# Head norms with tokens on the partitions, a new order of steps, and a regrouped recurrent mixer, in a two-layer streaming encoder trunk

## The chip, the cores and the metric

One core of a Trainium2 chip runs the whole program in one launch. The metric is the device time in microseconds (us) from start to end of one execution. Engines: TensorE (PE; its weight loads are shown as PEld), VectorE (DVE), ScalarE (ACT), GpSimd (POOL) and SyncE (SP), whose queue issues nearly all transfers.

## The reference, cut to what matters

Input is x of 512 tokens by 1024 channels. Two layers follow; each is half a SwiGLU feed-forward block (width 2816), a mixer, and another half block, all behind an RMS norm. The first layer's mixer ("even") runs eight attention heads of 64 beside eight RWKV-7 heads of 64; the second's ("odd") is a Griffin recurrent block of width 1280.

```python
for l in range(DEPTH):                       # DEPTH = 2
    x = x + 0.5 * swiglu(rmsnorm(x, ...), ...)
    h = rmsnorm(x, norm_mix[l])
    if l % 2 == 0:
        oa = chunk_attention(qa, ka, va, att_rel_bias[i])
        ob, v_b = rwkv7_group(pb, ...)
        x = x + jnp.concatenate([oa, ob], axis=-1) @ ab_w_out[i]
    else:
        x = x + rglru_block(h, ...)
    x = x + 0.5 * swiglu(rmsnorm(x, ...), ...)

# rwkv7_group, the two norms over the 64 channels of a head:
kk = _heads(k * k_k)
kk = kk * lax.rsqrt(jnp.maximum(jnp.sum(kk * kk, axis=-1, keepdims=True), 1e-24))
...
var = jnp.mean(jnp.square(o - mean), axis=-1, keepdims=True)
o = (o - mean) * lax.rsqrt(var + GN_EPS)
o = (o * ln_w + ln_b + jnp.sum(rh * kh * r_k, axis=-1, keepdims=True) * vh) * g

# rglru_block:
gate, xb = jnp.split(h @ w_in, 2, axis=-1)
gate = gelu(gate);  xc = conv4(xb) + conv_b
r = sigmoid(xc @ wa + ba);  ig = sigmoid(xc @ wx + bx)      # block-diagonal
a = exp(-8 * r * softplus(-lam));  mult = sqrt(1 - a * a)
hs = scan of  h_t = a_t * h_(t-1) + mult * ig * xc
return (hs * gate) @ w_out
```

## The kernel before, in words

**Layout.** Activations stand transposed: channels on the 128 partitions, the 512 tokens along the free axis, so a tile is 128x512. Every large product is made of three matmuls in a faster float format, on a high part and a remainder of each operand (`mm3`); the parts come from `split`: ScalarE copies the high part, VectorE subtracts it. Small products in the even mixer are plain float32 and appear as two matmul records each.

**Order of the program.** The phases are feed-forward 0, the even mixer (`ab`), feed-forward 1 and 2, the odd mixer (`rglru`), feed-forward 3. The compiler's planner orders each engine's instructions by program order and by when its model holds them ready. In the two mixers each TensorE instruction is pinned behind the one traced before it (`te.on`), so there TensorE's order is the written one, and the planner orders the other engines alone. Engines run their own queues in order. A tile's next use waits until the readers of the last one are done: PSUM has four banks under the name `mm` (projections, attention scores, transposes, outputs) and four under `aux` (small products).

**RMS norms.** `norm_square` squares each of the eight tiles of x and adds them up; `norm_end` sums over the partitions with a matmul of ones (`rms`), takes the root on ScalarE and the reciprocal on VectorE (`rsqrt`, lines 237 and 238). For the very first norm the squares are on GpSimd (line 222) and `norm_end` is called before the first feed-forward block; all other squares are on ScalarE (line 224).

**Even mixer.** Heads are worked in four pairs, numbers 0 to 3. Four strings give the written order: KEYS and VALUES (input projections, with the pairs' key preparation between), LEVELS (inverses of the triangular blocks) and ORDER (attention and the recurrence). A letter and a digit name a step and its pair; a number feeds so many units of a dense queue (in the first three the rest of the input projections, in ORDER the first half of the output projection), a unit being three 512-column matmuls; `k1:` feeds until that projection is done. The steps that matter here:

- `D` decay (line 532 on): LoRA products, sigmoids, a scan, exponentials; GpSimd forms `kah` from `a` (562), then VectorE turns `a` into (a-1)*k_a (563).
- `N` in KEYS (`pair_norm`, 573): one matmul of the squares with `blk`, a 128x128 matrix of two 64x64 blocks of ones, so that every partition of a head holds its sum (`kkn`); root, reciprocal of 128x512, then three VectorE products.
- `M` products of keys (`pair_lmat`), copied under a mask by VectorE (line 906); `T` token transposes of v; in ORDER `T`, `P`, `w`, `U`, `k`, `s`, `z`, `R`, `q`, `W` are the chunked recurrence of a pair.
- `N` in ORDER (`rwkv_norm`, 1070): matmul `gn_var` of the squares with `blk`, root (a table load and 512 columns on ScalarE), reciprocal, two VectorE products, GpSimd's product with the gate, and the split into `ob` (`mixed`).
- `A` and `B` (`att_probs`): scores of query blocks 0, 1 and 2, 3, each score tile in its own `mm` bank; reduction with the bias (line 711), exponential (717), reciprocal and scaling (720, 722). `B` ends with loading the next pair's query and key stacks. `C`, `E` (`att_turn`): transposes of the probabilities, copied back by ScalarE (735). `O`, `Y` (`att_out`): the products with v; `Y` ends with the split into `oa`.

**Odd mixer.** A loop of twenty projections (i = 0 to 19): ten give the branch that is convolved (`rg_conv`), ten the gate. Three projections later come that block's gates (`rg_gates`, sigmoids at line 1140). After the loop, for blocks 0 to 4 and then 5 to 9: tanh, exponential and square on ScalarE (1174 to 1177), two VectorE steps, then the root (1183), b = bx*m on GpSimd (1184), the scan on VectorE (1185), then GELU (1187), the product with the state (1188) and the split. The planner may start any of it earlier. The output projection (`cout`) follows, 240 matmuls.

Of the kernel before, what the change touches and what calls it, by code (L numbers as in the profile page):

```python
# [74 lines left out]
class Trunk:  # L75
# [3 lines left out]
    def __init__(self, ctx, tc, ins, out, first):  # L79
# [11 lines left out]
        self.n = 0  # L91
        self.jobs, self.parts_of, self.turn = [], {}, 0


# [157 lines left out]
    def ffn(self, li, next_gain):  # L252

        nc, tc = self.nc, self.tc
        wgu, wd = self.ins["gu"], self.ins["down"]
        xh, xl, rs = self.xh, self.xl, self.rs
        with tc.tile_pool(name=f"ffn{li}", bufs=1, reuse_waits="tile") as fp:
# [9 lines left out]
            for f in range(NF):  # L267
                pss = [self.mm_ps("gu") for _ in range(2)]
                both, at = [(0,), (1,)], None
                if self.early:  # L270


                    both, at = [(0, 1)], hbig.rearrange("p (a b) n -> p a (b n)", b=2)[:, 2:4]
                for ss in both:
                    parts = []
                    for s in ss:
                        place = at if s == 0 else None
                        parts.append(self.weights(wgu[li, f, s], D, at=None if place is None else (at[:, 0], at[:, 1])))
                    for k in range(KD):
                        c = slice(k * P, (k + 1) * P)  # L280
                        for s, (wh, wl) in zip(ss, parts):
                            self.mm3(
                                pss[s], wh[:, c], wl[:, c], xh[:, k], xl[:, k], k == 0, k == KD - 1
                            )
                g = fp.tile([P, NT], F32, tag="g", name=self.uid("g"), bufs=2)
# [40 lines left out]
    def ab(self, next_gain):  # L326
# [7 lines left out]
        with tc.tile_pool(name="ab", bufs=1, reuse_waits="tile") as rp:  # L334
# [3 lines left out]
            self.qkd = self.dp.tile([4, 2, 2, P, NT], F32, name="qkd")  # L338
            self.dec, self.kv, self.kk, self.vv, self.rr, self.pairs = ({} for _ in range(6))
            right = ExitStack()  # L340
            with tc.tile_pool(name="ab_in", bufs=1, reuse_waits="tile") as ep:
                self.later = None
                self.mtd = ep.tile([P, 32, 32], F32, tag="blocks", name="mtd")
                with tc.tile_pool(name="ab_keys", bufs=1, reuse_waits="tile") as kp:
# [15 lines left out]
                        "D": lambda p: self.rwkv_decay(p, rp, ep, kp),  # L360
                        "N": self.pair_norm,
                        "M": self.pair_lmat,
                        "T": lambda p: self.value_tokens(p, rp),
# [17 lines left out]
            with ExitStack() as st:  # L381
# [26 lines left out]
                    "W": lambda p: self.rwkv_out(p, sp),  # L408
                    "N": lambda p: self.rwkv_norm(p, rp),
                    "A": lambda p: self.att_probs(p, (0, 1), ap),  # L410
# [3 lines left out]
                    "O": lambda p: self.att_out(p, (0, 1)),  # L414
                    "Y": lambda p: self.att_out(p, (2, 3), rp),
                })
# [109 lines left out]
    def rwkv_decay(self, p, rp, ep, kp):  # L526
# [35 lines left out]
        nc.gpsimd.tensor_tensor(kah, a, kh, ALU.mult)  # L562
        nc.vector.tensor_scalar(a, a, -1.0, self.v("k_a", p), ALU.add, ALU.mult)
        self.dec[p] = kkt, rt, kh, kah, a
# [8 lines left out]
    def pair_norm(self, p):  # L573
        nc = self.nc
        kkt, rt, kh, kah, a = self.dec[p]
        k, kk, f = self.kv[p], *self.kk[p]
        ps = self.aux_ps("kkn")
        self.te.matmul(ps, self.blk, f, start=True, stop=True)
        self.rsqrt(f, ps, 1.0, 0.0)

        nc.vector.scalar_tensor_tensor(kk, f, 1e12, kk, ALU.min, ALU.mult)
        nc.vector.tensor_tensor(kkt, kk, kkt, ALU.mult)
        nc.vector.scalar_tensor_tensor(kah, kk, -1.0, kah, ALU.mult, ALU.mult)

    def pair_lmat(self, p):
# [5 lines left out]
        for q in range(4):  # L591
            q = slice(32 * q, 32 * q + 32)
            nc.scalar.activation(self.mtd[q, us], self.mt[q, us, q], AF.Copy)
        nc.vector.scalar_tensor_tensor(k2, k2, 1.0, self.kv[p], ALU.add, ALU.mult)
        nc.gpsimd.tensor_tensor(kh, k2, kh, ALU.mult)
# [92 lines left out]
    def att_probs(self, p, js, ap):  # L688
# [49 lines left out]

    def att_out(self, p, blocks, rp=None):

# [5 lines left out]
        for i in blocks:  # L746
            for h in range(2):
# [3 lines left out]
                )  # L751
        if rp:
            self.oa.append(self.mixed(rp, po, f"oa{p}"))

# [326 lines left out]

# [63 lines left out]
    def rglru(self, next_gain):  # L1145
        nc, tc = self.nc, self.tc
        self.te.on = True
        with tc.tile_pool(name="rg", bufs=1, reuse_waits="tile") as cp:
# [3 lines left out]
            rs_, bxs, ms, gs, yh, yl = [], [], [], [], [], []  # L1152
            convs = {}
            for i in range(2 * NR):
                n = i % NR
# [15 lines left out]
            for grp in (range(0, 5), range(5, 10)):  # L1171
                for n in grp:
                    m, a = slot("m", n), rs_[n]
                    nc.scalar.activation(m, a, AF.Tanh, scale=pos[:, n : n + 1])
                    nc.scalar.activation(a, a, AF.Exp, scale=neg[:, n : n + 1])
                    a2 = tmp("a2", 1)
                    nc.scalar.activation(a2, a, AF.Square)
                    nc.vector.tensor_scalar(a2, a2, 1.0, None, ALU.add)

                    nc.vector.scalar_tensor_tensor(m, m, 0.0, a2, ALU.max, ALU.mult)  # L1180
                    ms.append(m)
                for n in grp:
                    nc.scalar.activation(ms[n], ms[n], AF.Sqrt)
                    nc.gpsimd.tensor_tensor(bxs[n], bxs[n], ms[n], ALU.mult)
                    nc.vector.tensor_tensor_scan(bxs[n], rs_[n], bxs[n], 0.0, ALU.mult, ALU.add)  # L1185
                for n in grp:
                    nc.scalar.activation(gs[n], gs[n], AF.Gelu_apprx_tanh)
                    nc.vector.tensor_tensor(gs[n], gs[n], bxs[n], ALU.mult)
                    h, l = slot("r", n, F32R), slot("m", n, F32R)
                    self.split(h, l, gs[n])  # L1190
                    yh.append(h)
                    yl.append(l)
            self.norm_begin(next_gain)
# [85 lines left out]
def trunk_kernel(ctx: ExitStack, tc: tile.TileContext, ins: dict, out: bass.AP, phases="0A12C3"):  # L1279
# [97 lines left out]
```

## Time and profile before

| what | value |
|---|---|
| device time, median of 3 runs | 2000.65 us (1997.07 to 3977.45) |
| the profiled execution | 2000.92 us; its span 1999.2 us, 24418 instructions |
| TensorE busy | 1965.6 us (98%) |
| VectorE, ScalarE, GpSimd busy | 991.7, 770.3, 294.7 us (50, 39, 15%) |
| mean granted TensorE clock | 0.990 |
| HBM traffic | 258.30 MB read, 80.22 MB written |

The span is the time from the first to the last instruction. A busy TensorE is not TensorE at its peak: matmuls overlap, and a window's granted clock says which share of the full 2.4 GHz it had. "Idle before" is the time an engine did nothing before an instruction, and the name behind the arrow is the work whose end released it, as inferred from semaphores. Feed-forward 0 runs from 5 to 373 us, the even mixer to 720, feed-forward 1 and 2 to 1440, the odd mixer to 1626.

### The profile page before, as it was taken

Reading aid. Unit: us, or ns where it says so; the run is one execution under the profiler, and the core shown is the slowest. Engines: PE = TensorE matmul, PEld = TensorE weight load, DVE = VectorE, ACT = ScalarE, POOL = GpSimd, SP = SyncE. Lnnn points to the kernel's source line nnn. Section 1 sums busy time; section 2 is a strip of 40 time slices with the busy share of each in tenths; the row PEclk is TensorE's granted clock in tenths of the full one; section 3 lists DMA queues with packets and bytes.
Section 4 is the critical chain, followed back from the end, with each engine's and each line's share of the span. In section 5 each row is a group of like instructions: output and inputs, shape, how many; then the busy total and the mean of one; then the engine's idle time right before and its main releaser. Section 6 shows DMA issues by size and latency. Waiting matters only on the chain.

```text
span 1999.2 us, 24418 instructions
## 1 busy us (share of the span) xinstructions
PE 1965.6 (98%) x9642; PEld 1609.8 (81%) x9642; DVE 991.7 (50%) x1306; ACT 770.3 (39%) x1055; POOL 294.7 (15%) x216
## 2 busy tenths in 40 slices
PE   8999999999998999999999999999999999999998
PEld 6888888768776788888888888888888788888887
DVE  7655633378556465543335654433386544434332
ACT  5444422462245244422224442322279333222222
POOL 3111101112010021111000111101021211111100
PEclk9999999999998999999999999999999999999999
DMA  7999833534643469933335873233455442233332
GB/s 274 320 333 341 337 120 117 177 138 177 215 128 118 153 212 340 327 114 97 89 99 193 283 262 98 95 92 101 143 186 186 134 159 95 95 97 102 89 95 71
DMA packets 108930, 340.12 MB, mean 170 GB/s; under 512 B 12432, under 2 KB 15376, under 8 KB 108816
## 3 DMA queue, kind: packets, MB, share of 16 engines
q1 hardware_dynamic: 108672, 338.48, 50.2%
q8 instruction: 75, 1.23, 0.3%
q14 instruction: 39, 0.32, 0.1%
q10 hardware_dynamic: 144, 0.09, 0.0%
HBM read 258.30 MB, written 80.22 MB: 169 GB/s over the span
## 4 chain that ended last, share of the span: by engine, by line
PE 85%; DVE 7%; ACT 5%; issue 1%; DMA 1%; POOL 1%; SPq 0%; DVEq 0%; ACTq 0%; POOLq 0%
PE gu L69 47%; PE down L69 24%; PE proj L69 4%; PE cout L69 3%; PE outp L69 2%; DVE xc L1117 1%; PE prod L69 1%; DMA qkd<-qk 1%; DVE bx L1185 1%; DVE xblk L807 1%; DVE tblk L803 1%; PE wkv L69 1%; PE att_s L69 0%; ACT L1140 0%; PE w L69 0%
## 5 line engine op out<-in xcount | busy, mean ns | idle before, releaser
L141 ACT ACTIVATE whi<-raw 128x1024 fp32r<-128x1024 f32 (+2 forms) x269 | 277.6, 1032 | 787.9 <-PE gu L69 418.2
L69 PE MATMUL gu<-xh,wlo 128*128 128x512 f32 x1400 | 545.9, 390 | 1.0 <-DVE wlo L142 1.0
L69 PE MATMUL gu<-xl,whi 128*128 128x512 f32 x1400 | 545.5, 390 | 0.0
L69 PE MATMUL gu<-xh,whi 128*128 128x512 f32 x1400 | 545.5, 390 | 0.0
L142 DVE TENSOR_TENSOR wlo<-raw,whi 128x1024 fp32r<-128x1024 f32 (+2 forms) x269 | 322.8, 1200 | 243.5 <-ACT whi L141 240.2
L69 PEld LDWEIGHTS gu<-xh,wlo 128*128 128x128 f32 x1400 | 263.2, 188 | 56.6 <-DVE wlo L142 2.3
L69 PEld LDWEIGHTS gu<-xh,whi 128*128 128x128 f32 x1400 | 263.3, 188 | 54.8
L69 PEld LDWEIGHTS gu<-xl,whi 128*128 128x128 f32 x1400 | 263.2, 188 | 54.7
L289 POOL TENSOR_TENSOR s<-s,rs 128x512 f32<-128x512 f32 x88 | 153.9, 1749 | 801.7 <-ACT s L288 801.7
L69 PE MATMUL down<-hl,whi 128*128 128x512 f32 x558 | 217.2, 389 | 0.0
L69 PE MATMUL down<-hh,wlo 128*128 128x512 f32 x558 | 217.2, 389 | 0.0
L69 PE MATMUL down<-hh,whi 128*128 128x512 f32 x558 | 217.2, 389 | 0.0
L291 DVE TENSOR_TENSOR h<-gu,s 128x512 f32<-128x512 f32 x88 | 60.7, 690 | 207.8 <-PE gu L69 195.3
L286 DVE TENSOR_TENSOR g<-gu,rs 128x512 f32<-128x512 f32 x88 | 60.6, 690 | 164.1 <-PE gu L69 164.0
L227 POOL TENSOR_TENSOR ss<-ss,sq 128x512 f32<-128x512 f32 x36 | 53.7, 1492 | 486.7 <-ACT sq L224 486.7
L69 PEld LDWEIGHTS down<-hh,wlo 128*128 128x128 f32 x558 | 104.8, 188 | 21.7
L69 PEld LDWEIGHTS down<-hh,whi 128*128 128x128 f32 x558 | 104.8, 188 | 21.7
L69 PEld LDWEIGHTS down<-hl,whi 128*128 128x128 f32 x558 | 104.8, 188 | 21.6
L142 DVE TENSOR_TENSOR praw<-praw,phi 128x1024 f32<-128x1024 f32 (+2 forms) x75 | 87.2, 1164 | 58.7 <-ACT phi L141 58.0
L69 PE MATMUL proj<-xh,praw 128*128 128x512 f32 x336 | 114.0, 402 | 0.0
L141 ACT ACTIVATE phi<-praw 128x1024 fp32r<-128x1024 f32 (+2 forms) x75 | 72.1, 962 | 99.7 <-DMA praw<-in_cin_dram 39.8
L69 PE MATMUL down<-hbig,whi 128*128 128x512 f32 x248 | 76.9, 391 | 0.0
(439 smaller groups left out, 2329.0 us busy)
## 6 DMA issues: line engine op xcount, KB each, us to landing
raw<-in_gu_dram SPq DMA_DIRECT2D x174, 512.0 KB, 4.3
raw<-in_down_dram SPq DMA_DIRECT2D x64, 448.0 KB, 3.3
raw<-in_down_dram SPq DMA_DIRECT2D x32, 512.0 KB, 3.5
praw<-in_cin_dram SPq DMA_DIRECT2D x20, 512.0 KB, 5.4
parts_cin<-phi SPq DMA_DIRECT2D x20, 512.0 KB, 3.9
parts_cin<-praw SPq DMA_DIRECT2D x20, 512.0 KB, 5.1
praw<-parts_cin SPq DMA_DIRECT2D x20, 512.0 KB, 3.8
praw<-in_rw_dram SPq DMA_DIRECT2D x14, 512.0 KB, 6.1
```

What stands on the lines that cost most here:

```text
L69: return self.keep(self.tc.nc.tensor.matmul(*a, **k))
L141: nc.scalar.activation(hi, src, AF.Copy)
L142: (lo_eng or nc.vector).tensor_tensor(lo, src, hi.bitcast(F32), ALU.subtract)
L227: eng.tensor_tensor(self.ss, self.ss, sq, ALU.add)
L286: nc.vector.tensor_tensor(g, pss[0], rs, ALU.mult)
L289: nc.gpsimd.tensor_tensor(s, s, rs, ALU.mult)
L291: nc.vector.tensor_tensor(h, pss[1], s, ALU.mult)
L803: nc.vector.tensor_tensor(t, l[:, j + 1 :, j : j + 1].to_broadcast([P, n, c]), x[:, j : j + 1, 0:c].to_broadcast([P, n, c]), ALU.mult,)
L807: nc.vector.tensor_tensor(x[:, j + 1 :, 0:c], x[:, j + 1 :, 0:c], t, ALU.add)
L1117: nc.vector.scalar_tensor_tensor(xc, xb[:, w : w + NT], self.v("conv_w", 10 * w + n), xc, ALU.mult, ALU.add)
L1185: nc.vector.tensor_tensor_scan(bxs[n], rs_[n], bxs[n], 0.0, ALU.mult, ALU.add)
```

## The change

- *Head norms.* `head_sums` puts tokens on the partitions: four matmuls, the squares of 128 tokens as the stationary operand and two columns of `blk` as the moving one, give 128x8 sums. Root and reciprocal run over 8 columns. `head_rows` brings the result back: eight matmuls with one column of the 128x8 tile, broadcast to 64, as the stationary and the identity as the moving operand. Each norm becomes two steps: `N` (sums, root, reciprocal) and `J` (rows and products). The split into `ob` is a step of its own, `V`, and that into `oa` another, `X`.
- *Orders.* KEYS, VALUES, LEVELS and ORDER are new. In `D`, (a-1)*k_a moves to `M`.
- *Scores.* In `A`, blocks 0 and 1 of a head share one bank.
- *First norm.* The squares are on ScalarE; `norm_end` is called in the first feed-forward block, behind its first 48 matmuls.
- *Odd mixer.* The five blocks' states are placed in the loop, after i = 7 and after i = 12, each GELU from i = 13 on; the product with m moves to VectorE; `a2` has two buffers.

```diff
-ORDER = "A0 T0 B0 w0 R0 U0 P1 k0 A1 T1 s0 C0 E0 w1 z0 B1 q0 O0 W0 R1 N0 U1 Y0 P2 C1 k1 A2 T2 E1 s1 B2 w2 z1 q1 O1 W1 R2 N1 U2 Y1 P3 C2 k2 A3 T3 E2 s2 B3 w3 z2 q2 O2 W2 R3 N2 U3 Y2 C3 k3 E3 s3 O3 z3 Y3 q3 W3 5 N3"
+ORDER = "A0 P1 T0 B0 w0 R0 U0 E0 k0 A1 T1 C0 s0 P2 w1 z0 B1 q0 W0 O0 R1 N0 Y0 U1 J0 X0 C1 k1 E1 A2 s1 q1 B2 O1 z1 T2 Y1 W1 R2 N1 w2 V0 X1 J1 C2 T3 U2 V1 P3 k2 w3 E2 q2 A3 O2 s2 B3 z2 Y2 W2 U3 R3 k3 N2 C3 J2 E3 X2 s3 O3 Y3 X3 2 z3 q3 V2 W3 20 N3 5 J3 65 V3 11"
-KEYS = "7 n0 12: 13: k0: D0 k1: N0 D1 v0: 4 k2: M0 N1 D2 v1: T0 k3: M1 N2 D3 v2: T1 r0: M2 N3 v3: T2 r1: M3"
-VALUES = "r2: T3 r3: G0 G1 av: G2 G3 q0: 4"
-LEVELS = "Z0 Z1 4 Z2 Z3 4 Y0 Y1 4 Y2 Y3 4 X0 X1 4 X2 X3 4 W0 W1 4 W2 W3 4 P0 q3:"
+KEYS = "7 n0 13 12: 13: k0: D0 k1: N0 D1 v0: 11 J0 k2: 6 N1 M0 6 D2 T0 4 v1: J1 N2 4 k3: 1 M1 1 v2: 5 J2 1 D3 N3 4 r0: 3 v3: 3 T1 J3 M2 T2 3 r1: M3 4"
+VALUES = "5 T3 G0 G1 r2: 1 r3: 4 G2 20 G3 18 av: 4 q0: 6"
+LEVELS = "Z2 Z3 Z0 Z1 8 Y0 Y1 7 Y2 Y3 8 X0 X1 X2 4 W0 2 W2 3 W1 X3 3 W3 P0 q3: 36"
...
-        if first:
-            nc.gpsimd.tensor_tensor(sq, self.x[k], self.x[k], ALU.mult)
-        else:
-            nc.scalar.activation(sq, self.x[k], AF.Square)
+        nc.scalar.activation(sq, self.x[k], AF.Square)
...
+    def head_sums(self, sq):
+        ps = self.aux_ps("sums")
+        for j in range(4):
+            self.te.matmul(
+                ps[:, 2 * j : 2 * j + 2], sq[:, j * P : j * P + P], self.blk[:, 0:P:64],
+                start=True, stop=True,
+            )
+        return ps
+
+    def head_rows(self, f):
+        ps = self.aux_ps("rows")
+        for j in range(4):
+            for h in range(2):
+                self.te.matmul(
+                    ps[64 * h : 64 * h + 64, j * P : j * P + P],
+                    f[:, 2 * j + h : 2 * j + h + 1].to_broadcast([P, 64]), self.ident,
+                    start=True, stop=True,
+                )
+        return ps
...
+                if self.rs is None:          # in ffn, behind a block's matmuls
+                    self.te.on = True
+                    self.norm_end()
+                    self.te.on = False
...
     def pair_norm(self, p):
-        ps = self.aux_ps("kkn")
-        self.te.matmul(ps, self.blk, f, start=True, stop=True)
-        self.rsqrt(f, ps, 1.0, 0.0)
-        nc.vector.scalar_tensor_tensor(kk, f, 1e12, kk, ALU.min, ALU.mult)
-        nc.vector.tensor_tensor(kkt, kk, kkt, ALU.mult)
-        nc.vector.scalar_tensor_tensor(kah, kk, -1.0, kah, ALU.mult, ALU.mult)
+        n = self.nf[p] = self.cp.tile([P, 8], F32, tag="nf", name=self.uid("nf"), bufs=2)
+        self.rsqrt(n, self.head_sums(self.kk[p][1])[:, 0:8], 1.0, 0.0)
+        nc.vector.tensor_scalar(n, n, 1e12, None, ALU.min)
+
+    def pair_keys(self, p):                  # J in KEYS
+        ps = self.head_rows(self.nf[p])
+        nc.vector.tensor_tensor(f, ps, kk, ALU.mult)
+        nc.vector.tensor_tensor(kkt, f, kkt, ALU.mult)
+        nc.vector.scalar_tensor_tensor(kah, f, -1.0, kah, ALU.mult, ALU.mult)
...
-        for j in js:
+        for h, j in [(h, j) for h in range(2) for j in js] if js[0] == 0 else [(h, j) for j in js for h in range(2)]:
             n = (j + 1) * P
-            for h in range(2):
-                ps = pss[h, j] = self.mm_ps("att_s")
+            if True:
+                if j % 2 == 0 or j > 1:
+                    bank = self.mm_ps("att_s")
                 c = slice(0, max(n, 256))
+                ps = pss[h, j] = bank[:, 256 * j :] if j < 2 else bank
...
-    def rwkv_norm(self, p, rp):
-        ps = self.aux_ps("gn_var")
-        self.te.matmul(ps, self.blk, q, start=True, stop=True)
-        self.rsqrt(q, ps, 1.0 / 64, self.gneps)
-        nc.vector.scalar_tensor_tensor(o, o, self.v("ln_w", p), q, ALU.mult, ALU.mult)
+    def rwkv_norm(self, p):
+        n = self.nf[p] = self.cp.tile([P, 8], F32, tag="nf", name=self.uid("nf"), bufs=2)
+        self.rsqrt(n, self.head_sums(q)[:, 0:8], 1.0 / 64, self.gneps)
+
+    def rwkv_gate(self, p):                  # J in ORDER
+        ps = self.head_rows(self.nf[p])
+        nc.vector.scalar_tensor_tensor(o, o, self.v("ln_w", p), ps, ALU.mult, ALU.mult)
         nc.vector.scalar_tensor_tensor(o, o, self.v("ln_b", p), rkv, ALU.add, ALU.add)
         nc.gpsimd.tensor_tensor(o, o, g, ALU.mult)
-        self.ob.append(self.mixed(rp, o, f"ob{p}"))
...
+            def states(grp):                 # in rglru; the body as before, but
+                    a2 = tmp("a2", 2)
+                    nc.vector.tensor_tensor(bxs[n], bxs[n], ms[n], ALU.mult)
-                    a2 = tmp("a2", 1)
-                    nc.gpsimd.tensor_tensor(bxs[n], bxs[n], ms[n], ALU.mult)
...
+                if i == 7:
+                    states(range(0, 5))
+                elif i == 12:
+                    states(range(5, NR))
+                if i >= 13:
+                    gelus(range(max(0, i - NR + 1 - 1) if i > 13 else 0, i - NR + 2 - 1))
+            gelus(range(NR - 1, NR))
...
-    t.norm_end()                             # in trunk_kernel, ahead of the phases
```

## Rows read from the trace of the kernel before

**Rows 1.** The page, part 1: busy time, share of the span, instructions.

```profile
...
PE 1965.6 (98%) x9642; PEld 1609.8 (81%) x9642; DVE 991.7 (50%) x1306; ACT 770.3 (39%) x1055; POOL 294.7 (15%) x216
...
```

**Rows 2.** Waits of TensorE: engine line <- releaser: us in total, times, longest us.

```profile
...
PE att_s L69 <- ACT probs L735: 6.1, 2, 3.0
PE cout L69 <- ACT r L141: 3.2, 2, 1.8
PE a_lora L69 <- DVE mt L906: 2.9, 1, 2.9
PE att_s L69 <- DVE st L711: 2.3, 2, 1.2
PE rms L69 <- ACT ssp L141: 2.2, 1, 2.2
PE lv2z L69 <- ACT xu L858: 1.8, 1, 1.8
...
```

**Rows 3.** Windows: stretch, length; PE, PEld, DVE, ACT, POOL busy us (instructions); clock; DMA.

```profile
...
5.00:29.00 24.00, 19.73 (x70) 13.63 (x70) 21.91 (x24) 13.22 (x18) 10.57 (x7) 0.93 0.70 266
395.00:425.00 30.00, 27.10 (x104) 17.53 (x104) 19.64 (x23) 21.40 (x33) 5.52 (x5) 0.89 0.33 123
530.00:540.00 10.00, 8.16 (x150) 6.54 (x149) 3.79 (x8) 2.09 (x5) 0.95 (x1) 1.00 0.83 266
555.00:680.00 125.00, 112.32 (x1024) 91.63 (x1023) 73.67 (x194) 61.58 (x147) 13.04 (x13) 0.92 0.37 119
1450.00:1566.00 116.00, 116.00 (x512) 95.95 (x511) 86.84 (x119) 95.24 (x118) 29.80 (x28) 1.00 0.54 177
1566.00:1628.00 62.00, 58.41 (x238) 45.68 (x237) 19.00 (x27) 15.58 (x23) 8.30 (x6) 0.94 0.52 170
...
```

**Rows 4.** Chain that ended last, in order of time: start us, us, what.

```profile
...
253.42 119.68 PE down L69 x528
...
378.32 0.79 PE rst L69 x8
...
```

**Rows 5.** The same chain, round of pair 1's head norm.

```profile
...
628.76 1.07 PE gn_var L69 x2
629.89 1.28 ACT L237
631.91 3.35 DVE q L238
...
637.87 1.28 POOL o L1079
641.26 1.28 ACT L717
...
645.22 2.32 PE att_s L69 x8
...
```

**Rows 6.** Line 238, reciprocal: count, ns min/median/max, first and last start us.

```profile
...
L238 DVE RECIPROCAL q<-q x4: 3352/3352/3353, 601.2 to 679.6; 128x512 f32<-128x512 f32 x4
L238 DVE RECIPROCAL rstf<-rstf x2: 165/166/166, 1983.2 to 1993.3; 128x2 f32<-128x2 f32 x2
...
```

**Rows 7.** Timeline of TensorE, output products: start us, us, operation, count.

```profile
...
623.70 0.39 PE L69 MATMUL wkv<-tok,vt 128*64 128x128 f32 x4
623.92 0.39 PE L69 MATMUL wkv<-tok,ug 128*64 128x128 f32 x4
...
```

**Rows 8.** Timeline of VectorE in the keys; brackets: idle before, releaser.

```profile
...
414.37 0.49 DVE L563 TENSOR_SCALAR a<-a,vec 128x512 f32<-128x512 f32 x1 [3.35 <-POOL kah L562]
...
418.31 1.33 DVE L906 COPY_PREDICATED mt<-mask,prod 128x512 f32<-128x512 uint32 x2
```

**Rows 9.** Line 224, squares on ScalarE, columns as in rows 6.

```profile
...
L224 ACT ACTIVATE sq<-xb x34: 614/616/633, 704.9 to 1972.9; 128x512 f32<-128x512 f32 x34
...
```

**Rows 10.** Groups by line, 1438 to 1576 us: busy us, mean ns | idle before.

```profile
...
L1184 POOL TENSOR_TENSOR bx<-bx,m 128x512 f32<-128x512 f32 x10 | 15.7, 1588 | 26.8 <-ACT m L1183 26.8
...
L1175 ACT ACT_TABLE_LOAD x10 | 12.8, 1283 | 0.2
...
L1188 DVE TENSOR_TENSOR g<-g,bx 128x512 f32<-128x512 f32 x10 | 6.7, 683 | 9.4 <-ACT g L1187 9.4
...
```

More of the change, by code (lines that the diff above doesn't have):

```diff
@@ L92, in __init__ @@
         self.jobs, self.parts_of, self.turn = [], {}, 0
+        self.rs = None
         warm = self.cp.tile([P, NT], F32, tag="sq", name="warm", bufs=2)
@@ L255, in ffn @@
         wgu, wd = self.ins["gu"], self.ins["down"]
-        xh, xl, rs = self.xh, self.xl, self.rs
+        xh, xl = self.xh, self.xl
         with tc.tile_pool(name=f"ffn{li}", bufs=1, reuse_waits="tile") as fp:
@@ L284, in ffn @@
                             )
+                if self.rs is None:
+                    self.te.on = True
+                    self.norm_end()
+                    self.te.on = False
+                rs = self.rs
                 g = fp.tile([P, NT], F32, tag="g", name=self.uid("g"), bufs=2)
@@ L338, in ab @@
             self.qkd = self.dp.tile([4, 2, 2, P, NT], F32, name="qkd")
-            self.dec, self.kv, self.kk, self.vv, self.rr, self.pairs = ({} for _ in range(6))
+            self.dec, self.kv, self.kk, self.vv, self.rr, self.pairs, self.nf = ({} for _ in range(7))
             right = ExitStack()
@@ L361, in ab @@
                         "N": self.pair_norm,
+                        "J": self.pair_keys,
                         "M": self.pair_lmat,
@@ L408, in ab @@
                     "W": lambda p: self.rwkv_out(p, sp),
-                    "N": lambda p: self.rwkv_norm(p, rp),
+                    "N": self.rwkv_norm,
+                    "J": self.rwkv_gate,
+                    "V": lambda p: self.ob.append(self.mixed(rp, self.wkv[p][0], f"ob{p}")),
+                    "X": lambda p: self.oa.append(self.mixed(rp, self.att[p][2], f"oa{p}")),
                     "A": lambda p: self.att_probs(p, (0, 1), ap),
@@ L414, in ab @@
                     "O": lambda p: self.att_out(p, (0, 1)),
-                    "Y": lambda p: self.att_out(p, (2, 3), rp),
+                    "Y": lambda p: self.att_out(p, (2, 3)),
                 })
@@ L562, in rwkv_decay @@
         nc.gpsimd.tensor_tensor(kah, a, kh, ALU.mult)
-        nc.vector.tensor_scalar(a, a, -1.0, self.v("k_a", p), ALU.add, ALU.mult)
         self.dec[p] = kkt, rt, kh, kah, a
@@ L574, in pair_norm @@
         nc = self.nc
-        kkt, rt, kh, kah, a = self.dec[p]
-        k, kk, f = self.kv[p], *self.kk[p]
-        ps = self.aux_ps("kkn")
-        self.te.matmul(ps, self.blk, f, start=True, stop=True)
-        self.rsqrt(f, ps, 1.0, 0.0)
-        nc.vector.scalar_tensor_tensor(kk, f, 1e12, kk, ALU.min, ALU.mult)
-        nc.vector.tensor_tensor(kkt, kk, kkt, ALU.mult)
-        nc.vector.scalar_tensor_tensor(kah, kk, -1.0, kah, ALU.mult, ALU.mult)
+        n = self.nf[p] = self.cp.tile([P, 8], F32, tag="nf", name=self.uid("nf"), bufs=2)
+        self.rsqrt(n, self.head_sums(self.kk[p][1])[:, 0:8], 1.0, 0.0)
+        nc.vector.tensor_scalar(n, n, 1e12, None, ALU.min)
+    def pair_keys(self, p):
+        nc = self.nc
+        kkt, rt, kh, kah, a = self.dec[p]
+        kk, f = self.kk[p]
+        ps = self.head_rows(self.nf[p])
+        nc.vector.tensor_tensor(f, ps, kk, ALU.mult)
+        nc.vector.tensor_tensor(kkt, f, kkt, ALU.mult)
+        nc.vector.scalar_tensor_tensor(kah, f, -1.0, kah, ALU.mult, ALU.mult)
     def pair_lmat(self, p):
@@ L593, in pair_lmat @@
             nc.scalar.activation(self.mtd[q, us], self.mt[q, us, q], AF.Copy)
+        nc.vector.tensor_scalar(k2, k2, -1.0, self.v("k_a", p), ALU.add, ALU.mult)
         nc.vector.scalar_tensor_tensor(k2, k2, 1.0, self.kv[p], ALU.add, ALU.mult)
@@ L737, in att_turn, with att_out @@
                 )
-    def att_out(self, p, blocks, rp=None):
+    def att_out(self, p, blocks):
         hs = [slice(0, 64), slice(64, 128)]
@@ L751, in att_out @@
                 )
-        if rp:
-            self.oa.append(self.mixed(rp, po, f"oa{p}"))
     def mixed(self, rp, o, name):
@@ L1153, in rglru, with gelus @@
             convs = {}
+            act = lambda *a, **k: nc.scalar.activation(*a, **k)
+            def states(grp):
+                for n in grp:
+                    m, a = slot("m", n), rs_[n]
+                    act(m, a, AF.Tanh, scale=pos[:, n : n + 1])
+                    act(a, a, AF.Exp, scale=neg[:, n : n + 1])
+                    a2 = tmp("a2", 2)
+                    act(a2, a, AF.Square)
+                    nc.vector.tensor_scalar(a2, a2, 1.0, None, ALU.add)
+                    nc.vector.scalar_tensor_tensor(m, m, 0.0, a2, ALU.max, ALU.mult)
+                    ms.append(m)
+                for n in grp:
+                    act(ms[n], ms[n], AF.Sqrt)
+                    nc.vector.tensor_tensor(bxs[n], bxs[n], ms[n], ALU.mult)
+                    nc.vector.tensor_tensor_scan(bxs[n], rs_[n], bxs[n], 0.0, ALU.mult, ALU.add)
+            def gelus(grp):
+                for n in grp:
+                    act(gs[n], gs[n], AF.Gelu_apprx_tanh)
+                    nc.vector.tensor_tensor(gs[n], gs[n], bxs[n], ALU.mult)
+                    h, l = slot("r", n, F32R), slot("m", n, F32R)
+                    self.split(h, l, gs[n])
+                    yh.append(h)
+                    yl.append(l)
             for i in range(2 * NR):
@@ L1170, in rglru @@
                     gs.append(g)
[L1171 to L1175, printed above, removed]
-                    a2 = tmp("a2", 1)
[L1177 to L1183, printed above, removed]
-                    nc.gpsimd.tensor_tensor(bxs[n], bxs[n], ms[n], ALU.mult)
[L1185 to L1192, printed above, removed]
+                if i == 7:
[5 more added lines that the diff above has]
+            gelus(range(NR - 1, NR))
             self.norm_begin(next_gain)
```

1 line of the change is left out of this document (added).

## The prediction

> **What bounds the kernel now.** I read the busy times first. TensorE is busy for 1965.6 of 1999.2 us [rows 1], so only what TensorE loses or is spared can move the time; the other engines matter where TensorE waits for them. The list of TensorE's waits says where that is [rows 2]: attention scores waiting for the transposed probabilities' copies (6.1 us) and for score banks (2.3), the output projection of the recurrent mixer waiting for its last gated tiles (3.2), a LoRA product behind a masked copy (2.9), the first norm's sum (2.2), one inverse level (1.8). Idle time is half of it: the windows around these waits also show a granted clock below 1.0 [rows 3], because stretches after a wait run at 1.2 instead of 2.4 GHz. So I price a stretch by idle time plus the share of clock missing; in stretches that are all 512-column matmuls, by their count times 119.68/528 = 0.227 us each [rows 4]. Least time that could be given back, stretch by stretch [rows 3]:
>
> - start, 5 to 29 us: 24.0 - 70 x 0.227 = **8.1**
> - keys, 395 to 425: idle 2.9, clock 0.11 x 30 = 3.3: **6.2**
> - inverse levels, 530 to 540: **1.8**
> - mixing order, 555 to 680: idle 12.7, clock 0.08 x 125 = 10.0: **22.7** (a little too much, where the two overlap)
> - end of the recurrent mixer, 1566 to 1628: 62.0 - 238 x 0.227 = **8.0**
>
> Together 46.8 us, 2.3% of the span. Nothing else of the four feed-forward blocks is touched. Changes of under 2% (40 us) either way count as no change here, so the question is whether nearly all of the 46.8 comes back.
>
> **Head norms.** Today one 128x128 by 512 matmul sums the squares, ScalarE takes 512 roots and VectorE 512 reciprocals. The chain of one pair shows the price [rows 5]: the matmul at 628.76, a table load at 629.89, the reciprocal at 631.91 for 3.35 us, GpSimd's gate product at 637.87, the next table load only at 641.26, exponentials, and TensorE takes up the scores at 645.22. Eight such reciprocals (four in the keys, four in the mixing) take 3.35 us each [rows 6]. In the new form they are over 8 columns; the nearest row is one of 2 columns, 0.17 us [rows 6], so VectorE loses 3.2 us per pair, and copies of products and score reductions queued behind it come earlier. On TensorE it costs more than before. Four sum matmuls with one 128-column stationary each: 0.79 us, from four of that form [rows 4]. Eight spreading matmuls, each 64 wide and 128 columns: two of that form start every 0.22 us, the two halves of the partitions side by side [rows 7], so 0.87. Against 1.07 before [rows 5] this is +0.59 us per norm, **+4.7** for eight. If the halves don't overlap it is 8 x 0.22 = 1.74, +1.46 each, +11.7: the high bound; 0 would be the low one if all hid behind waits. I take +4.7, since the partition halves alternate here as in that row.
>
> The Trainium skill, "TensorE: Matmul & The Clock Gate", section "Wait — 56ns, not 53.3ns?", has about 62 ns as the largest fixed floor of a tiny matmul. The four sums, two passes each, would then cost about 0.5 us (an estimate from that page) and the eight norms +2.4 in all, 2.3 us less than by the row; the row (99 ns per pass) decides.
>
> TensorE keeps program order in the mixing, so a new wait appears at each spreading step. Behind it stand the next pair's products and transposes, so it has to be covered by what lies between sums and spreading. In the keys that is ten or more feeds of three 512-column matmuls, over 6.8 us. In the mixing it is thin: for pair 1 only one step of 16 small matmuls, for pair 2 one group of 14 transposes, about 2 us, against a table load of 1.28 [rows 5], a root and a reciprocal of 0.17 each or a little more, and queueing. I charge 0.7 us for each of three pairs, **+2**.
>
> **New orders.** Keys: at 414.37 VectorE has stood 3.35 us before "less one, times k_a" of pair 1, because GpSimd still reads that tile [rows 8]; the masked copy that holds TensorE is queued behind it. The change moves this step from the decay to the product step, where GpSimd is long done, drops the reciprocal that made the decay late, and puts pair 2's decay several feeds later. I take **-5.5** of 6.2 (0 if the copy waits for something else next). Levels: the first second-level step waits 1.8; eight feeds now stand before it: **-1.8** (0 if the copies are still late). Mixing: the 6.1 us of rows 2 come from copies behind a table load behind the reciprocal chain of rows 5. With the chain shorter, the later transposes moved before the next scores, two score blocks sharing a bank (two banks for four matmul groups instead of four) and the splits of the outputs put off, most of this should go. Not all: score step B still takes all four banks and output step O comes right after it, and three pairs' thin covers are new. Bounds 0 and 22.7; I take two thirds, **-15.5**, nearer the top because each wait listed hangs on the chain that is cut. The queue of transfers is hardly disturbed: gate and bonus loads of pair 1 now come after the spreading of pair 0 by about 5 us of TensorE work, and the stacks of the next pair are asked for after score step B as before, some 18 us ahead of use.
>
> **Start.** Eight squares go from GpSimd to ScalarE, 0.62 each [rows 9], 5.0 us on an engine busy 13.2 of 24 [rows 3]; VectorE, busy 21.9 of 24, no longer runs beside GpSimd's squares. The norm's sum is pinned behind the first block's matmuls, not ahead. The wait of 2.2 and the low clock around it (0.07 x 24 = 1.7) should go and about 1 us of the smaller waits: **-5** of 8.1. The low bound is 0: if ScalarE's squares come after the weight splits, the same wait returns.
>
> **Recurrent mixer.** Before, ScalarE is busy 95.2 of 116 us from 1450 on [rows 3], with a table load of 1.28 for every one of the ten exponentials [rows 10], because roots, sigmoids, exponentials and GELUs alternate; so the last tiles come after the projections end. Now five blocks' states stand together at the eighth projection, five at the thirteenth, and each GELU right after its projection. ScalarE then works in a few long groups, done before the last projection. The last tile's chain is four passes of about 0.7 (product, GELU, product, split and its remainder), 3.5 us; TensorE has nine blocks of three matmuls before it needs that tile, 27 x 0.227 = 6.1. The product with m moves from GpSimd, 1.59 [rows 10], to VectorE at 0.68 as its neighbour's: +6.8 on an engine busy 86.8 of 116 [rows 3]. I take **-7** of 8.0. By the new loop's bounds the last tile is gated and split twice; the second split can only be written when the output projection has read the first. It is read by nobody, so I cost it at nothing; four passes, 2.6 us, if it delays the next norm.
>
> **Sum.** -5 - 5.5 - 1.8 - 15.5 - 7 + 4.7 + 2 = -28.1. The profiled execution took 2000.92 us (span 1999.2), 0.3 above the median of the runs, 2000.65. 2000.9 - 28.1 = **1973 us**.
>
> **Rivals.** (1) *Everything comes back*: all 46.8, with +4.7: 1959. For it: every listed wait is named by something the change moves. Against: small waits in the mixing are many, and the new form adds some. 10%. (2) *The mixing trades its waits*: banks of score step B or the thin covers hold TensorE as long as before; only the mixing's gain is lost: 1988. For it: ScalarE and VectorE are still busy about half of that stretch [rows 3], and a table load stands in each norm as before. 18%. (3) *VectorE becomes the bound in the recurrent mixer*: between the eighth and thirteenth projection it has the convolutions of three blocks, three gate products and five blocks' states, about as much as TensorE has matmuls; the gain of 7 is lost and about 5 added by projections waiting for a bank: 1985. 7%. (4) *Slower*: TensorE stands at each spreading step because the root waits in ScalarE's queue behind exponentials or copies. Price as in the keys' wait now, 2.9 idle and 3.3 of clock, 6.2 each, eight times 49.6: 2022. It decides from 28.1/8 = 3.5 us per norm. Against: in the keys the cover is over 6.8 us. 5%. (5) *It doesn't do what it says*: the written order binds TensorE alone, and the planner, which orders ScalarE and VectorE by itself, goes on alternating tables in the recurrent mixer: 1980. 3%.
>
> **Numbers.** Forecast 57%, 1973, with 1965 to 1982 for its own terms. The range 1958 to 1993 takes in rivals 2, 3 and 5 and most of 1, and the higher price of the spreading matmuls (+7). Faster than 1960.6 needs nearly all of rival 1: 0.06. Slower than 2040.7 needs rival 4 at more than its price: 0.02. Within: 0.92.
>
> **What would show it.** In the profile after: no reciprocal of 512 columns in the two norms; sum and spreading groups of about 0.8 and 0.9 us; fewer table loads in the recurrent mixer and no wait of the output projection; no wait of the scores for the transposed copies; a granted clock of 1.0 from 395 to 425. A wait at the spreading matmuls of over 3 us, or scores waiting for banks, would prove me wrong.

## The result, and the profile after

The changed kernel takes **1965.54 us**, median of 4 runs (1964.6 to 1965.85); the kernel before, run beside it, 1999.68 (4 runs). The ratio is 0.9836 [0.9819, 0.9853], 34 us less: a real gain, and within the 2% that counts as no change. The forecast was 1973. Between the two profiled executions the span fell by 36.3 us (1999.2 to 1962.9), where the forecast's sum was 28.1.

Busy times on the page after, which answer to [rows 1]:

```profile
...
PE 1951.9 (99%) x9818; PEld 1607.1 (82%) x9818; DVE 966.3 (49%) x1322; ACT 763.9 (39%) x1058; POOL 267.2 (14%) x198
...
```

TensorE has 176 instructions more and is busy 13.7 us less. Its waits after (engine, line and releaser: us in total, times, longest), against [rows 2]:

```profile
PE gu L69 <- ACT hbig L142: 1.6, 2, 1.0
PE warm L69 <- DVE warm L97: 1.5, 1, 1.5
PE rst L69 <- ACT sq_last L1304: 0.8, 1, 0.8
...
PE att_s L69 <- ACT probs L771: 0.2, 1, 0.2
...
```

All six waits of [rows 2] are gone but for 0.2 us, and none stands at the spreading matmuls (`rows`). The windows around the same work, in the columns of [rows 3]:

```profile
5.00:29.00 24.00, 22.30 (x93) 17.11 (x94) 21.84 (x27) 19.90 (x29) 0.00 (x0) 1.00 0.91 337
385.00:440.00 55.00, 55.00 (x302) 41.58 (x302) 29.97 (x50) 35.39 (x57) 8.47 (x7) 1.00 0.41 148
...
552.00:669.00 117.00, 116.39 (x1160) 97.27 (x1160) 66.45 (x199) 58.94 (x146) 14.60 (x14) 1.00 0.47 153
1421.00:1537.00 116.00, 116.00 (x511) 95.62 (x510) 93.71 (x138) 91.24 (x118) 14.55 (x18) 1.00 0.53 177
1537.00:1592.00 55.00, 55.00 (x238) 44.28 (x237) 14.25 (x19) 12.50 (x20) 8.31 (x6) 1.00 0.59 190
...
```

The granted clock is 1.00 in each, so a wait that went took its slow stretch along. By stage, cut at TensorE's first instruction of each (worked out from the two traces; the forecast's norm cost is put where it falls):

| stage | before, us | after, us | change | forecast |
|---|---|---|---|---|
| up to the even mixer's first projection | 372.94 | 367.45 | -5.49 | -5.0 |
| its keys and levels | 189.69 | 185.05 | -4.64 | -4.95 |
| mixing order | 157.53 | 137.92 | -19.61 | -11.15 |
| feed-forward 1 and 2 | 719.45 | 719.93 | +0.48 | 0 |
| odd mixer | 186.23 | 179.48 | -6.75 | -7.0 |
| feed-forward 3 | 373.35 | 373.05 | -0.30 | 0 |

Five of the six came out within 0.5 us of their terms. The mixing gave 8.5 us more than forecast, which is the whole miss. One profiled execution further down, that of the grouping alone, ran at a low clock throughout; its times aren't used.

### The profile page after: what moved, and what is told of

It reads as the page before. It is cut to its first block, busy times and chain, and to the rows that moved or that the text cites. A ratio compares the mean times of both kernels' runs of the same rounds, so it can differ in the third digit from the quotient of the medians.

```text
span 1962.9 us, 24783 instructions
## 1 busy us (share of the span) xinstructions
PE 1951.9 (99%) x9818; PEld 1607.1 (82%) x9818; DVE 966.3 (49%) x1322; ACT 763.9 (39%) x1058; POOL 267.2 (14%) x198
## 4 chain that ended last, share of the span: by engine, by line
PE 95%; DMA 2%; DVE 1%; ACT 0%; issue 0%; SPq 0%; POOL 0%; DVEq 0%; ACTq 0%
PE gu L69 46%; PE down L69 24%; PE proj L69 12%; PE cout L69 3%; PE outp L69 2%; PE vproj L69 1%; PE prod L69 1%; PE rggate L69 1%; DMA praw<-in_cin_dram 1%; DMA parts_cin<-praw 1%; PE wkv L69 1%; PE att_o L69 0%; PE att_s L69 0%; DMA parts_gates<-praw 0%; PE rows L69 0%; PE ug L69 0%
```

## The experiments

Two theories: **R**, the gain in keys and mixing comes from the short chain of the new head norms; **O**, it comes from the new order of the steps. The first run puts the new norms into the kernel before, each `J` right behind its `N`.

```diff
-... R1 N0 U1 Y0 P2 ...    KEYS: k1: N0 D1 v0: 4 ...
+... R1 N0 J0 U1 Y0 P2 ... KEYS: k1: N0 J0 D1 v0: 4 ...
```

> The kernel before with the new head norms alone, old orders; the spreading step J stands right behind the sums N. Theory R (the 512-column root and reciprocal held the old order back): the keys and the mixing lose their waits (about -6 and -17 us), the norms cost +6, and TensorE waits at each J for a table load, a root and a reciprocal of 8 columns, about 2.2 us, eight times +18: about 2001 us. Theory O (the written order was the cause, the reciprocal not): the old waits stay and the new ones are added: about 2024 us. If a wait at J costs 6 us, as rival 4 of the prediction priced it, it is slower still: 2032 or more.

2018.03 us, ratio 1.0107 [1.0078, 1.0136]: slower by 1.1%, between the totals of the two theories. TensorE's waits (line 602 is in the keys, 260 in the mixing):

```profile
PE rows L69 <- DVE nf L602: 10.8, 4, 3.1
PE att_s L69 <- ACT probs L763: 6.6, 2, 3.3
...
PE rows L69 <- DVE nf L260: 2.7, 4, 0.7
...
```

Without cover, the spreading matmuls stand 2.7 us per norm in the keys and 0.7 in the mixing, and the keys grow from 145.1 to 159.4 us, of which 13.7 run at half clock (1.2 GHz) where 6.8 did before. That is the mechanism of rival 4. The short reciprocal doesn't prevent it: in pair 0's norm a table load of 1.28 us comes first, and then the root's result lies 1.0 us behind two VectorE products before the reciprocal of 0.20 starts. The scores' wait is not touched.

The second run keeps the old order and puts each `J` some steps behind.

```diff
+... R1 N0 U1 Y0 J0 P2 ... KEYS: k1: N0 D1 v0: J0 4 ...
```

> As e1, but J stands some steps behind N: in the mixing behind the second output step Y of the pair, in the keys behind the next value projection. Theory R: the mixing falls from 157.7 us to 140 to 146, the keys by 3 to 5, nothing waits at J: about 1983 us. Theory O: the mixing stays at 157 or more, the whole at 2000 or above.

1998.09 us, ratio 1.0008 [0.9995, 1.0021]: nothing gained. The keys have no wait any more (143.4 us), but the mixing takes 161.1 (in a profiled execution 6 us above the median) and the scores wait as before, with 8-column reciprocals:

```profile
PE att_s L69 <- ACT probs L763: 6.6, 2, 3.3
```

R falls for the mixing. The mirror image is the changed kernel with the old norm: matmul with `blk`, root and reciprocal of 512 columns at `N`, products at `J`.

```diff
-        self.rsqrt(n, self.head_sums(q)[:, 0:8], 1.0 / 64, self.gneps)
+        ps = self.aux_ps("gn_var")
+        self.te.matmul(ps, self.blk, q, start=True, stop=True)
+        self.rsqrt(q, ps, 1.0 / 64, self.gneps)
```

> The changed kernel with the old norms (one matmul with the block matrix, root and reciprocal of 512 columns) at N, and the products at J; everything else as changed. Theory R: the mixing goes back from 138 us to about 150, the whole to about 1977. Theory O: TensorE saves about 6 us of norm matmuls and no wait comes back: about 1959 us, below the changed kernel's 1965.5.

1960.53 us, ratio 0.9821 [0.9807, 0.9836]: 5.0 us *below* the changed kernel. In keys and mixing the order gives all of the gain, and the head norm in its new form costs time. The odd mixer's grouping alone, on the kernel before, product still on GpSimd:

```diff
+                if i == 7:
+                    states(range(0, 5))
+                elif i == 12:
+                    states(range(5, NR))
```

> The kernel before with the odd mixer's new grouping alone, the product with m left on GpSimd. Theory G (states ahead of the GELUs is what frees the end): the odd mixer falls from 186.2 to about 180 us and the whole to about 1993. Theory M (the product on GpSimd, which slows the scan beside it, is what made the end late): the odd mixer stays at 184 or more, the whole at 1998 or more.

1996.13 us, ratio 0.9983 [0.9966, 1.0]: 2 to 3 us less, too near to none to settle it. The two runs on the odd mixer further down do.

Next, what in the order of the mixing does it. Undone in the changed kernel, the shared bank:

```diff
-                if j % 2 == 0 or j > 1:
-                    bank = self.mm_ps("att_s")
+                bank = self.mm_ps("att_s")
```

> The changed kernel with a bank of its own for every score tile, as before. Theory B (score banks: four of them taken by A keep the transposes and the next scores out): waits of the scores come back, the mixing goes from 137.9 to 145 or more, the whole to 1972 or more. Theory E (the place of the later transposes E, ahead of the next scores, is the cause): the mixing stays within 3 us, the whole at 1964 to 1968.

1965.6 us, ratio 0.9835 [0.981, 0.986]: no difference. The shared bank alone in the kernel before (the scores then go head by head, as in the changed kernel):

```diff
-                ps = pss[h, j] = self.mm_ps("att_s")
+                if j % 2 == 0 or j > 1:
+                    bank = self.mm_ps("att_s")
+                ps = pss[h, j] = bank[:, 256 * j :] if j < 2 else bank
```

> The kernel before with blocks 0 and 1 of a head in one score bank, all else old. Theory B: the wait of the scores for the copies (6.1 us) goes and with it most of the low clock: mixing 157.5 to about 143, the whole about 1985. Theory E: only the 2.3 us of waits for banks go: mixing about 154, the whole about 1996.

1999.26 us, ratio 1.0002 [0.9985, 1.0019]. The wait of 2.3 us for score banks in [rows 2] goes. The scores' wait for the copies stays, and TensorE stands in two new places:

```profile
PE att_s L69 <- ACT probs L737: 5.4, 2, 2.7
...
PE att_t L72 <- DVE oa0l L142: 1.9, 1, 1.9
PE att_t L72 <- DVE oa1l L142: 1.9, 1, 1.9
```

Now three letters moved in the kernel before, and nothing else: `E` of pairs 0 to 2 goes ahead of the next pair's `A`.

```diff
-... k0 A1 T1 s0 C0 E0 w1 ... k1 A2 T2 E1 s1 ... k2 A3 T3 E2 s2 ...
+... k0 E0 A1 T1 s0 C0 w1 ... k1 E1 A2 T2 s1 ... k2 E2 A3 T3 s2 ...
```

> The kernel before with step E (transposes of the later blocks) moved ahead of the next pair's A for pairs 0 to 2, all else old, the 512-column norm too. Theory E: ScalarE copies E's tiles before A's exponentials, B finds its banks free: mixing 157.5 to about 143, the whole about 1985. Theory B, or the splits' place: the wait moves to A or B's banks, the mixing stays above 152, the whole above 1994.

1982.4 us (1981.77 to 1984.14), ratio 0.9922 [0.99, 0.9943]. The mixing falls from 157.5 to 137.2 us, within 1 us of the changed kernel's, with the old 512-column norm. The two ScalarE timelines of the round of pair 1's head norm, in which `E` of pair 2, `A` and `B` of pair 3 follow, show why. Before (start us, us; the scores that wait are the last row of [rows 5], at 645.22):

```profile
640.66 0.60 ACT L935 ACTIVATE tok<-tok 128x512 f32<-128x512 f32 x1
641.26 1.28 ACT L717 ACT_TABLE_LOAD   x1
...
644.33 0.57 ACT L935 ACTIVATE tok<-tok 128x512 f32<-128x512 f32 x1
644.80 0.96 ACT L735 ACTIVATE probs<-att_t 128x256 f32<-128x256 f32 x4
```

With `E` ahead:

```profile
626.90 1.08 ACT L735 ACTIVATE probs<-att_t 128x256 f32<-128x256 f32 x4 [0.95 <-PE att_t L72]
629.17 0.63 ACT L141 ACTIVATE ob1h<-o 128x512 fp32r<-128x512 f32 x1 [1.19 <-POOL o L1079]
...
631.28 1.28 ACT L717 ACT_TABLE_LOAD   x1
```

Before, TensorE ends `E`'s transposes at 641.92 (the last two start at 641.18 and take 0.74), but their copies stand in ScalarE's queue behind a table load, the next pair's first exponentials and a token copy until 644.80. `B`'s scores need the banks those copies empty. With `E` ahead, the copies are done at 627.98, 3.3 us before the table load, and `B`'s scores, from 630.57, follow without a gap. The splits, put back right behind `Y` and `J` in the changed kernel:

```diff
-... N0 Y0 U1 J0 X0 C1 ... w2 V0 X1 J1 C2 T3 U2 V1 P3 ...
+... N0 Y0 X0 U1 J0 V0 C1 ... w2 J1 V1 C2 T3 U2 P3 ...
```

> The changed kernel with the splits of the outputs back where they were (X right behind Y, V right behind J). If putting them off is what keeps VectorE and ScalarE free for the scores, waits come back and the mixing goes from 137.9 to 142 or more, the whole to 1970 or more. If the place of E or the banks is the cause, the mixing stays within 2 us and the whole at 1964 to 1968.

1966.26 us, ratio 0.9839 [0.9817, 0.986]: nothing. Then three small parts undone together, each in a stage of its own: first squares on GpSimd, (a-1)*k_a back in `D`, bx*m on GpSimd.

```diff
+            nc.gpsimd.tensor_tensor(sq, self.x[k], self.x[k], ALU.mult)
...
+        nc.vector.tensor_scalar(a, a, -1.0, self.v("k_a", p), ALU.add, ALU.mult)   # in D
...
-                    nc.vector.tensor_tensor(bxs[n], bxs[n], ms[n], ALU.mult)
+                    nc.gpsimd.tensor_tensor(bxs[n], bxs[n], ms[n], ALU.mult)
```

> The changed kernel with three parts undone, each in a stage of its own: first squares on GpSimd (norm_end still behind the first block), (a-1)*k_a back in the decay step, the product with m back on GpSimd. Start: if the engine of the squares is the cause, feed-forward 0 goes from 361.6 to 365 or more; if the place of norm_end is, it stays below 363. Keys: if VectorE's wait at (a-1)*k_a for GpSimd is the cause, a wait of about 3 us comes back and the stage goes from 144.2 to 147 or more; if the new order is, it stays within 1. Odd mixer: if the grouping is the cause, its 179.5 stay within 1; if the product on GpSimd is, 183 or more.

1975.56 us, ratio 0.9878 [0.9865, 0.9892], 10 us above the changed kernel. Waits:

```profile
PE rggate L69 <- ACT bx L1180: 2.5, 1, 2.5
...
PE rms L69 <- ACT ssp L142: 2.2, 1, 2.2
```

The wait of `rms` is back in full, so the squares' engine was its cause. The keys stay at 144.22 us with no wait of TensorE, though VectorE stands behind GpSimd at (a-1)*k_a again (4.4 us over three pairs, 10.1 in the kernel before); so moving that step is not what keeps the wait away here. In the odd mixer GpSimd's product costs 2.5 us at another place, while `cout` waits for nothing. The opposite, on the kernel before: squares on ScalarE and bx*m on VectorE, the old grouping kept.

```diff
-            nc.gpsimd.tensor_tensor(sq, self.x[k], self.x[k], ALU.mult)
+            nc.scalar.activation(sq, self.x[k], AF.Square)
...
-                    nc.gpsimd.tensor_tensor(bxs[n], bxs[n], ms[n], ALU.mult)
+                    nc.vector.tensor_tensor(bxs[n], bxs[n], ms[n], ALU.mult)
```

> The kernel before with two parts of the change alone, in stages of their own: first squares on ScalarE (norm_end where it was) and the product with m on VectorE (old grouping). Start: engine of the squares 367.8 to 363 or less; place of norm_end 366 or more. Odd mixer: product on VectorE as cause 186.2 to 182 or less; grouping as cause 185 or more. Nothing else moves: 1989 us if both engines are the causes, 1998 if neither.

1989.36 us, ratio 0.9948 [0.993, 0.9967]. At the start the wait of `rms` is gone and feed-forward 0 (from TensorE's first product on) takes 363.4 us, 0.4 above what was expected if the squares' engine is the cause; that is 4.4 of the 6.2 us between 367.8 and 361.6. The 1.8 left over are about what 3.4 us at half clock cost early in this execution. In both kernels, in this run and in the one before, `rms` stands behind 58 or 59 products, so nothing shows a gain from the place of `norm_end`. The odd mixer takes 180.2 us, 6.0 of the 6.8 given back, without regrouping. With regrouping and GpSimd's product (the run before) it takes 182.0, 4.2 given back. Either takes away the `cout` wait (0.6 us of it left here); they don't add up.

Last, versions that beat both kernels. The changed kernel with the old norm and without the second gating of the last tile:

```diff
-            gelus(range(NR - 1, NR))
```

> The changed kernel with the old norms (as e3_after_old_norm) and without the second gating of the odd mixer's last tile. The norms cost TensorE about 5 us less than in the changed kernel and bring no wait back: 1960.5 us as in e3. If the second gating delayed the next feed-forward's norm, up to 2.6 us less: 1958.

1960.72 us, ratio 0.9803 [0.9789, 0.9816], against 1960.53 with it: it costs nothing. On top of that, the sums of squares in one pass: the squares are written in the large products' float format (a coarser rounding of the sums), and the root goes to a tile of its own.

```diff
-        self.te.matmul(ps, self.blk, q, start=True, stop=True)
-        self.rsqrt(q, ps, 1.0 / 64, self.gneps)
+        self.te.matmul(ps, self.blk_r, q, start=True, stop=True)
+        n = self.nf[p] = self.cp.tile([P, NT], F32, tag="sq", name=self.uid("nf"), bufs=2)
+        self.rsqrt(n, ps, 1.0 / 64, self.gneps)
```

> As e8, but the squares are written in the format of the large products and summed by the block matrix in one pass: one record of 512 columns in place of two float32 ones, about 0.23 us for 1.07, eight times: -6.7 us, about 1954. If VectorE's wide reciprocals become the bound once the matmuls are short, waits appear behind the norms and it stays at 1958 or more.

**1954.13 us** (1953.16 to 1955.18), ratio 0.9769 [0.9756, 0.9782]: the best, 11.4 us below the changed kernel. The sums, 8 records each for the four keys' and the four output norms before this edit, are now 4 each (groups, as in [rows 10]):

```profile
L69 PE MATMUL gn_var<-q,blk_r 128*128 128x512 f32 x4 | 1.9, 471 | 0.0
L69 PE MATMUL kkn<-kk,blk_r 128*128 128x512 f32 x4 | 1.8, 448 | 0.8 <-DVE mt L941 0.4 <-ACT e L570 0.4
```

The keys fall from 139.9 to 138.9 us and the mixing from 138.1 to 131.7. There TensorE's idle time (2.5 to 0.6) and half-clock time (3.4 to 0) go as well; which of the two edits took those away wasn't separated. So the -6.7 was met (-6.6), but not by its one term alone: in the keys new waits in front of the sums (0.8 us idle) took back a part, and in the mixing idle and half-clock time added to the shorter sums.

## Why the prediction came out as it did

**What bounds it: right.** Waits of TensorE and the slow clock after them were the whole matter; the stretches that were priced are the stretches that changed. The result lies at the lower edge of the 1965 to 1982 given for the forecast's own terms.

**Start: right in size, right in cause.** -5 forecast, -5.5 found; undoing the squares alone among the parts of that stage brings 2.2 us of wait back, and the squares alone in the kernel before take it away. The place of `norm_end`, which the forecast named beside them, isn't shown to matter.

**Keys: right in size, half right in cause.** I put the wait on VectorE standing behind GpSimd at (a-1)*k_a [rows 8]. With that step in its old place, in the second run and in the one with three parts undone, there is no wait. What takes it away is either the short reciprocal with its products some steps later, in the old order (143.4 us), or the new order with the wide reciprocal (139.95 us): in each the masked copy comes in time. Both stood in the forecast beside the step that isn't needed. Which part of the new order does it wasn't separated, and that step alone in the kernel before wasn't run. Keys and levels together came out at -4.6.

**Levels: not shown.** The wait of 1.8 us is gone after, but it is also missing from the waits of the shared bank alone, whose edit comes behind the levels. It differs between executions (2.1 us in the run with `E` ahead), so its going can't be put down to the eight feeds.

**Mixing: the step that failed.** "the 6.1 us of rows 2 come from copies behind a table load behind the reciprocal chain": the table load was right, the chain was not what had to be cut. With the chain cut and the order kept the wait is 6.6 us; with the chain kept and three letters moved it is gone. [Rows 5] show the reciprocal and the late scores on one path, and I read the longest piece of the path as its cause. The forecast did name the moved transposes, as one of four parts, and the shared bank and the splits, which do nothing here; it hung the size on the chain. ScalarE takes its queue in order, so what counted was what stood ahead of `E`'s copies. The doubt that went with it, "two thirds" of 22.7, was thus too careful: once the copies stand ahead, all of it comes back (19.6 net, and what the norms cost there comes on top).

**Head norms: right sign, mis-sized.** One norm after, in the chain of the changed kernel (start us, us), first in the keys, then in the mixing:

```profile
393.58 0.79 PE sums L69 x8
...
409.46 1.02 PE rows L69 x16
...
604.48 0.98 PE sums L69 x8
...
607.30 1.02 PE rows L69 x16
```

The old ones, in the chain of the changed kernel with the old norm:

```profile
393.64 0.86 PE kkn L69 x2
...
627.24 1.07 PE gn_var L69 x2
```

So by these pairs a norm costs 1.81 us against 0.86 in the keys and 2.00 against 1.07 in the mixing: about +0.94 each and +7.5 for eight, not +4.7. The spreading matmuls took 1.02, not 0.87; the sums took the 0.79 that I had from [rows 4] only outside the thick of the mixing; and I subtracted the 1.07 of [rows 5] from all eight. Between the kernels the difference is 5.0 us, 4.3 of it in the keys (144.22 against 139.95), since with the wide reciprocal the mixing keeps some waits (2.5 us idle against 0.6). The Trainium skill, "TensorE: Matmul & The Clock Gate", section "Wait — 56ns, not 53.3ns?", would have given the eight norms +2.4 (an estimate) with its floor of about 62 ns; the trace shows more than that floor, 0.79 us over eight records being 99 ns each.

**Thin covers: nothing.** I charged +2 for three pairs; no wait at `J` is listed. In pair 1's round above, 1.84 us of `w` matmuls lie between sums and rows, and that is enough. The first run shows the price when that cover is left out.

**Odd mixer: right in size, half right in cause.** -6.8 against -7. I put it on "a few long groups" of ScalarE. Table loads of the projections' stretch after (groups in the columns of [rows 10]):

```profile
L1191 ACT ACT_TABLE_LOAD x19 | 24.4, 1283 | 0.3
...
L1177 ACT ACT_TABLE_LOAD x9 | 11.5, 1283 | 0.2
```

That is 28 loads where there were 34 (the ten of [rows 10], ten more for the sigmoids, seven each for roots and GELUs), and ScalarE is still busy 91.2 of 116 us, before 95.2. What I costed only as a load on VectorE, taking the product off GpSimd, gives back 6.0 us alone, more than the grouping's 4.2: +6.9 us on VectorE against 6.8 forecast, and the scans behind it wait no longer and none of them is slow. The scan on VectorE before, as a group and (in the columns of [rows 6]) by its shortest, median and longest, and then after:

```profile
L1185 DVE TENSOR_TENSOR_SCAN bx<-r,bx 128x512 f32<-128x512 f32 x10 | 15.2, 1536 | 5.8 <-POOL bx L1184 5.8
...
L1185 DVE TENSOR_TENSOR_SCAN bx<-r,bx x10: 1194/1220/2312, 1474.5 to 1564.3; 128x512 f32<-128x512 f32 x10
```

```profile
L1207 DVE TENSOR_TENSOR_SCAN bx<-r,bx 128x512 f32<-128x512 f32 x10 | 12.2, 1219 | 0.1
```

The mean before hides two kinds: seven scans took 1194 to 1225 ns, and three, started between 1552 and 1559 us, shortly ahead of the output projection, took 2246 to 2312 beside GpSimd's products with m.

The second gating of the last tile cost nothing, as forecast: in ScalarE's timeline its split comes at 1590.77, after `cout` had read the first, while TensorE goes on.

**Rivals.** Rival 1 was nearest in the mixing, where everything came back; over the whole, some 44 of the 46.8 us did (36.3 and the norms' 7.5), and the norms' higher price kept the total away from its 1959. Rivals 2 and 3 didn't happen: no bank wait took the old one's place, and VectorE, busy 93.7 of 116 us, held nobody. Rival 4 is real, and is what the first experiment built; the spread of `N` and `J` avoids it. Rival 5 was partly so, as the tables went on alternating, at no cost.

The total was nearer than its reasons: the mixing without its norms gave some 23 us where -15.5 and the +2 of thin covers stood, a term about 10 too small, and a norm cost some 3 too small took part of that miss away. That was luck.

## What to carry to other kernels

When TensorE waits for a PSUM bank, look at what stands ahead of the emptying copy in its engine's own queue, not at the longest piece of the chain: here three letters in the order were worth 16 us, and eight shorter reciprocals less than nothing. A cheaper vector step bought with many small matmuls is a loss on a TensorE that is 98% busy, unless the vector step is what TensorE waits for; test that with the vector step put back alone. A new producer and consumer pair on an in-order engine needs work between its halves, and that work made the difference between 2018 and 1998 us.

## What the runs showed of the hardware

- The price of waits of the same total varies, by one profiled execution each. With 12.7, 12.8 and 12.6 us of idle time the mixing had 20.5, 10.2 and 13.7 us at half clock and took 157.5, 151.2 and 154.1 us (the kernel before, its shared-bank version, and the one with two small parts). All runs but two of the kernel before lie between 1993 and 2004 us, those of the best within about 2.
- A scan of 512 columns on VectorE took 2246 to 2312 ns where GpSimd's products with m ran beside it for 1.2 us or more (three of ten before), and 1194 to 1225 in the other seven, in all ten after, and in all ten with the product on VectorE in the kernel before. In the run with GpSimd's product and the new grouping one of ten took 2308.
- Few moving columns don't make a matmul cheap: four matmuls of a 128-column float32 stationary and 2 moving columns took 0.79 us, nearly as long as the one matmul of 512 moving columns that they replace (0.86).
